# Layer 1's gate product as three 256-column matmuls summed in one PSUM region, and one more probability buffer in the attention of a two-layer block

## The chip, the cores and the metric

The kernel runs on one core of a Trainium2 chip. The metric is the device time of one execution in microseconds, and the time of a kernel is the median of several executions. The engines are named as the profile names them: PE (TensorE, matmul), PEld (the loads of PE's stationary operand, which overlap its matmuls), DVE (VectorE), ACT (ScalarE), POOL (GpSimd) and SP (SyncE, which here only issues DMAs). Each engine works through its own instructions in order.

## The reference, cut to what matters

A block of two layers works on 256 tokens and on 256 context tokens of width 2048. Layer 0 is a Fourier mixer, and layer 1 is attention with a window, a sink and a gate. What the change touches is in layer 1:

```
q, k, v, z = jnp.split(h @ w_in, [D_BRANCH, D_BRANCH + kvw, D_BRANCH + 2 * kvw], axis=-1)
...
p = jax.nn.softmax(jnp.concatenate([s, sk], axis=-1), axis=-1)[..., :-1]
o = jnp.einsum('bhgqk,bkhd->bqhgd', p, v)
y = o.reshape(b, n, D_BRANCH) * jax.nn.silu(z)
x = x + gate * (y @ w_out[i])
```

`h` has 256 rows of 2048 numbers. `z` has 4096 columns. There are 64 heads of 64 columns each, and each head has 512 keys (256 of the sequence and 256 of the context) for 256 queries.

## The kernel before, in words

All weights come as float32 and are used in two parts. A cast on ACT (`wh`) keeps the high bits, and a subtraction on DVE (`wl`) keeps the rest; both parts have the type float32r. `half_split` (line 69) does that for a tile of 128 x 1024. The activations are kept in two parts in the same way: in layer 1, `hx1[k]` is a tile of 128 x 512 with the high part of 256 tokens in columns 0 to 255 and the low part in columns 256 to 511, for 16 tiles `k` of the 2048 inputs. A product in full precision is then three matmuls, high by high, high by low and low by high, which the helper `mm3` (line 144) issues; the product of the low parts is left out.

Layer 1's attention is one long loop over 66 slots (line 1556). Its parts are:

- `stage_s(i)` (line 1476) for head `i`. Per block `tb` of 128 queries, PE makes the scores (lines 1489 and 1490), DVE adds the mask and takes the maximum (line 1491), and ACT takes the exponential into `p` (line 1494). DVE makes the reciprocal of the sum. ACT then writes the high half of the scaled probabilities into `f` in float16 (line 1506), DVE writes the low half (line 1507), and SP issues a transposing DMA from `f` to `ft` (line 1509). There are two `f` and one `ft` per head; `f` has 3 buffers and `ft` has 3.
- `stage_o(i - 2)` (line 1519) for the head two slots earlier. PE multiplies the values with `ft` (lines 1524 and 1525), ACT copies the upper 64 rows to a small tile `ot` (line 1530, a tile of its own with one buffer), and DVE adds them to the lower 64 rows (line 1531).
- two fillers per slot, which are units of other matmul work taken from one list (`units`, line 1379). A unit is an eighth of a group's query product (`q`, 64 units), half of a gate block (`z`, 64 units for 32 blocks), or a part of the last output product (`o`, 14 units). Each unit needs one `half_split`, which is asked for one unit ahead (`prep`, line 1402), and there are six buffers for `wh` and `wl`.

A gate block `z` is 128 of the 4096 gate columns for 256 tokens. It is built from 16 tiles `k`. For each tile the kernel before issues two matmuls, which share one PSUM tile of 512 columns: `wh` against the whole `hx1[k]` (line 1451, 512 columns), so that high by high lands in columns 0 to 255 and high by low in columns 256 to 511, and `wl` against the high half (line 1453, 256 columns), which adds to columns 0 to 255. Behind the last tile the two halves are added: ACT copies the right half to a tile `zs` (line 1457), DVE adds the left half (line 1458), ACT takes a tanh (line 1459), and DVE makes the SiLU's product `th` (line 1460). `emit_y` (line 1466) multiplies that with the head's output.

The order of the work on each engine is fixed when the program is built. A planner takes the instructions as the source writes them, runs them through a timing model with the buffers that the pools have, and writes one list per engine. Tiles of one tag share the buffers of that tag, and the instruction that first writes a new tile waits for those that last used the buffer. The pool `act` (line 40) has 33 buffers of 128 x 512 and one common tag `act`: among others the tiles of the rotary step on POOL (lines 1132 to 1138), the 16 tiles `y1` and scratch tiles are taken from it.

Loads of weights (`raw`, line 47, 1 MB each, three buffers) and the transposing DMAs are both issued by SP, in one order. POOL's own work in this stage is the rotary step for the queries, the low part of the keys (line 1346), and a share of the splits of `y` (line 1274).

Of the kernel before, what the change touches and what calls it, by code (L numbers as in the profile page):

```python
# [10 lines left out]
F32 = mybir.dt.float32  # L11
F32R = mybir.dt.float32r
F16 = mybir.dt.float16
AF = mybir.ActivationFunctionType
ALU = mybir.AluOpType
AX = mybir.AxisListType

P = 128
D = 2048
KT = D // P  # L20
DB = 4096
NB = DB // P
N = 256
# [9 lines left out]
def tile_dit(ctx: ExitStack, tc: tile.TileContext, a: dict, out: bass.AP):  # L33
    nc = tc.nc
    V, S, PE, GP = nc.vector, nc.scalar, nc.tensor, nc.gpsimd
# [19 lines left out]
    def act(dt=F32):  # L55
        return actp.tile([P, 512], dt, tag="act", name="act")
# [87 lines left out]
    def mm3(o, wh, wl, xh, xl, start, stop):  # L144
        PE.matmul(o, wh, xh, start=start, stop=False)  # L145
        PE.matmul(o, wh, xl, start=False, stop=False)  # L146
        return PE.matmul(o, wl, xh, start=False, stop=stop).ins  # L147
# [491 lines left out]
    for g in range(G):  # L639
        for j in {13: (8, 9), 14: (10, 11)}.get(g, (g - 5,) if 5 <= g < 13 else ()):  # L640
            t = up.tile([P, 1024], F32, name="pz", tag="pz", bufs=1)
# [217 lines left out]
    with tc.tile_pool(name="yp", reuse_waits="tile", bufs=32) as ypool:  # L859
# [39 lines left out]
        if True:  # L899
# [21 lines left out]
            for kg in range(4):  # L921
# [10 lines left out]
                for j in range(4):  # L932
                    k = kg * 4 + j
                    wh, wl = w[j // 2]
                    for b in range(4):
                        q = slice((j % 2) * 512 + b * P, (j % 2) * 512 + (b + 1) * P)
# [7 lines left out]
            for b in range(4, NB):  # L944
# [9 lines left out]
                o = psum()  # L954
                for k in range(KT):
# [13 lines left out]
                    wh, wl = w[k // 8]  # L969
                    q = slice((k % 8) * P, (k % 8 + 1) * P)  # L970
# [60 lines left out]
        for i in range(32):  # L1031
            sw, kg = i // 16, i % 16
            if kg == 0:
                o = [psum() for _ in range(8)]
# [9 lines left out]
            if kg == 14:  # L1044
                q = gt0[:, sw * 8 : sw * 8 + 8].rearrange("p k s -> p (k s)")
# [12 lines left out]
            if kg >= 12:  # L1058
                for k in range(sw * 8 + (kg - 12) * 2, sw * 8 + (kg - 12) * 2 + 2):
                    t = act()  # L1060
# [6 lines left out]
            for j, b in [(j, b) for b in range(8) for j in range(2)] if edge else [(j, b) for j in range(2) for b in range(8)]:  # L1067
                q = slice(b * P, (b + 1) * P)
# [35 lines left out]
    with tc.issue_after(st_end[0]):  # L1104
        o = psum()
# [34 lines left out]
    with tc.tile_pool(name="h1", reuse_waits="tile", bufs=16) as h1p:  # L1140
        hx1 = []
# [3 lines left out]
        with tc.tile_pool(name="kvp", reuse_waits="tile", bufs=2) as kvp:  # L1145
# [4 lines left out]
            for k in range(KT):  # L1150
                z2 = kvp.tile([P, 1024], F16, tag="hz", name="hz", bufs=16)
                t = kvp.tile([P, 512], F32, tag="ht", name="ht")
                for s in range(2):
                    q = slice(s * N, (s + 1) * N)
# [40 lines left out]
            o = [[psum() for _ in range(2)] for _ in range(4)]  # L1195
            for kg in range(8):
# [16 lines left out]
                for j in range(2):  # L1213
                    k = kg * 2 + j
                    wh, wl = w[j]
                    for tb in range(4):
                        c = tb // 2 * 512 + tb % 2 * P
                        for kv in range(2):
                            q = slice(kv * 512, (kv + 1) * 512)
                            mm3(o[tb][kv], hz[k][:, c : c + P], hz[k][:, N + c : N + c + P], wh[:, q], wl[:, q], k == 0, k == KT - 1)  # L1220
            kr = []
            for tb in range(4):
                t, ab = act(), act(F32R)
# [3 lines left out]
                t = act()  # L1227
# [20 lines left out]
            for tb in range(4):  # L1248
                t = vs[tb][0]
# [10 lines left out]
        with tc.tile_pool(name="at", reuse_waits="tile", bufs=2) as at:  # L1260
# [152 lines left out]
            def emit_unit():  # L1413
                if pos[0] >= len(ulist):
                    return
                u = ulist[pos[0]]
                if pos[0] not in ready:
                    ready[pos[0]] = prep(u)
                if pos[0] + 1 < len(ulist):
                    ready[pos[0] + 1] = prep(ulist[pos[0] + 1])  # L1420
                w = ready.pop(pos[0])
                pos[0] += 1
                kind, n, i, o = u
                if kind == "o":
                    if n == 0:
                        oA.extend([psum(), psum()])
                    for j in range(2):
                        o1_step(n * 2 + j, oA, *(t[:, j * 512 : (j + 1) * 512] for t in w))
                    return
                wh, wl = w  # L1430
                if kind == "q":
                    if i == 0:
                        o += [psum(), psum()]
                    if (n, i) == (0, 4):
                        with tc.issue_after(last_cast[0]):
                            prep_kk(0)
                    for j in range(2):
                        k = i * 2 + j
                        q = slice(j * 512, (j + 1) * 512)
                        for tb in range(2):  # L1440
                            mm3(o[tb], hx1[k][:, tb * P : (tb + 1) * P], hx1[k][:, N + tb * P : N + (tb + 1) * P], wh[:, q], wl[:, q], k == 0, k == KT - 1)
                    if i == 7:
                        finish_q(n, o)
                else:
                    if i == 0:
                        o.append(psum())
                    for k in range(i * 8, i * 8 + 8):
                        q = slice((k % 8) * P, (k % 8 + 1) * P)
                        for part in (0, 1) if k < KT - 1 else (1, 0):
                            if part == 0:  # L1450
                                PE.matmul(o[0], wh[:, q], hx1[k], start=k == 0, stop=k == KT - 1)  # L1451
                            else:
                                PE.matmul(o[0][:, 0:N], wl[:, q], hx1[k][:, 0:N], start=False, stop=False)  # L1453
                    if i == 1:
                        th = at.tile([P, N], F32, tag="th", name="th", bufs=3)
                        zs = at.tile([P, N], F32, tag="zs", name="zs", bufs=1)
                        S.copy(zs, o[0][:, N : 2 * N])
                        V.tensor_tensor(zs, o[0][:, 0:N], zs, op=ALU.add)
                        S.activation(th, zs, AF.Tanh, scale=0.5)
                        V.scalar_tensor_tensor(th, th, 1.0, zs, op0=ALU.add, op1=ALU.mult)  # L1460
                        szs[n] = th
                        emit_y(n)
# [13 lines left out]
            def stage_s(i):  # L1476
                hk, blk, hh = i // 8, i // 2, i % 2
                p2, pr = (blk % 4) // 2, blk % 2
                kkh, kkl = kk[hk]
                q2 = qq[hk, p2][hh]  # L1480
                pt = [at.tile([P, 512], F32, tag="p", name="p", bufs=3) for _ in range(2)]
                mx = at.tile([P, 2], F32, tag="mx", name="mx")
                sm = at.tile([P, 2], F32, tag="sm", name="sm")
                es = at.tile([P, 2], F32, tag="es", name="es")
                so = []
                for tb in range(2):
                    o = psum()
                    st = q2[:, (pr * 2 + tb) * P : (pr * 2 + tb + 1) * P]
                    PE.matmul(o, st, kkh, start=True, stop=False)  # L1489
                    PE.matmul(o, st, kkl, start=False, stop=True)  # L1490
                    V.tensor_tensor_reduce(o, o, mask[:, tb, :], -0.125, nsink[:, i : i + 1], ALU.add, ALU.min, mx[:, tb : tb + 1])  # L1491
                    so.append(o)
                for tb in range(2):
                    S.activation(pt[tb], so[tb], AF.Exp, bias=mx[:, tb : tb + 1], scale=-1.0, accum_out=sm[:, tb : tb + 1])  # L1494
                S.activation(es, mx, AF.Exp, bias=sink[:, i : i + 1])
                V.scalar_tensor_tensor(sm, sm, 1.0 / PS, es, op0=ALU.mult, op1=ALU.add)
                V.reciprocal(sm, sm)
                ft = at.tile([P, 8, 2, P], F16, tag="ft", name="ft", bufs=3)
                fs = []
                for tb in range(2):  # L1500
                    if i < 61:
                        f = at.tile([P, 1024], F16, tag="f", name="f", bufs=3)
                    else:
                        f = actp.tile([P, 1024], F16, tag="act", name="f")
                        fs.append(f)
                    fa = S.activation(f[:, 0:512], pt[tb], AF.Copy, scale=sm[:, tb : tb + 1]).ins  # L1506
                    f_last[:] = fa, V.scalar_tensor_tensor(f[:, 512:1024], pt[tb], sm[:, tb : tb + 1], f[:, 0:512], op0=ALU.mult, op1=ALU.subtract).ins  # L1507
                    if i < 61:
                        nc.sync.dma_start_transpose(ft[:, :, tb, :], f)
                return ft, fs  # L1510
# [8 lines left out]
            def stage_o(i, ft, fs):  # L1519
                hk, blk, hh = i // 8, i // 2, i % 2  # L1520
                oo = psum()
                for kb in range(4):
                    fh, fl = (ft[:, j, :, :].rearrange("p t q -> p (t q)") for j in (kb, 4 + kb))
                    PE.matmul(oo[:, 0:N], v01[kb][:, hk, :], fh, start=kb == 0, stop=False)  # L1524
                    PE.matmul(oo[:, 0:N], v01[kb][:, hk, :], fl, start=False, stop=kb == 3)  # L1525
                if hh == 0:
                    obs[blk, 0] = at.tile([P, N], F32, tag="ob", name="ob", bufs=4)
                ob = obs[blk, 0]
                t = at.tile([64, N], F32, tag="ot", name="ot", bufs=1)
                S.copy(t, oo[64:128, 0:N])  # L1530
                V.tensor_tensor(ob[hh * 64 : hh * 64 + 64, :], oo[0:64, 0:N], t, op=ALU.add)
                if hh == 1:
                    obs[blk, 1] = ob
                    emit_y(blk)
# [21 lines left out]
            for i in range(66):  # L1556
# [3 lines left out]
                if i == 61:  # L1560
                    t = actp.tile([P, 1024], F16, tag="act", name="ident16")
# [15 lines left out]
        with tc.tile_pool(name="fin", reuse_waits="tile", bufs=1) as fp:  # L1577
# [42 lines left out]
            for kg in range(16):  # L1620
# [10 lines left out]
                for j in range(2):  # L1631
                    k = kg * 2 + j
# [188 lines left out]
```

## Time and profile before

| what | us |
|---|---|
| median of 3 runs | 1764.61 (1764.34 to 1765.5) |
| the profiled execution, its own time | 1766.34 |
| its span from the first to the last instruction | 1764.5 |
| PE busy | 1728.8 (98%) |
| DVE busy | 1421.9 (81%) |
| ACT busy | 1148.4 (65%) |
| first and last matmul of the gate product (line 1451) | 1142.7 and 1567.0 |

A row of a group gives the line, the engine, the operation, the tiles (out <- in), the sizes and the number of instructions. Behind the bar it gives the busy time and the mean length of one in ns, and behind the second bar the time that the engine was idle just before such an instruction, with what ended the idle time. A row of the timeline gives the start, the length, the engine, the line and the operation. Matmuls are pipelined: the length of one reaches to the modelled end of its results, so the next one starts earlier than that, and the rate of PE is read from starts and not from lengths.

### The profile page before, as it was taken

How to read it: one execution, taken by the hardware profiler on the slowest of the kernel's cores; microseconds unless marked ns; L12 is line 12 of the kernel's file. 1: busy time of each engine (PE TensorE's matmuls, PEld its weight loads, DVE VectorE, ACT ScalarE, POOL GpSimd, SP SyncE). 2: the span in 40 equal slices, each digit the busy share in tenths (PEclk: the TensorE clock that was granted, in tenths of full speed). 3: DMA queues.
4: the chain of work that ended last, by engine and by line, in shares of the span. 5: the costliest groups of instructions: out<-in, count | busy, mean ns of one | idle time of the engine just before them, and what ended most of it. 6: DMA issues, size and time to landing. Idle time of an engine off the chain costs nothing.

```text
span 1764.5 us, 26891 instructions
## 1 busy us (share of the span) xinstructions
PE 1728.8 (98%) x9539; PEld 1149.6 (65%) x9539; DVE 1421.9 (81%) x2475; ACT 1148.4 (65%) x2197; POOL 361.3 (20%) x485
## 2 busy tenths in 40 slices
PE   6999999999999999999999999999999999999998
PEld 4679999644444444446444745788888878877464
DVE  5769888798676787777698686899899889998755
ACT  5545556476777755465235596688888788897643
POOL 0002111211222105212311111412303221251001
PEclk9999999999999999999999999999999999999999
DMA  9998999778998869977996594688997897888643
GB/s 394 417 342 254 275 273 257 295 282 303 340 314 299 312 227 378 372 254 258 394 341 229 181 362 155 191 198 198 222 212 200 204 212 207 210 192 283 225 172 120
DMA packets 232296, 465.66 MB, mean 264 GB/s; under 512 B 154497, under 2 KB 154897, under 8 KB 205281
## 3 DMA queue, kind: packets, MB, share of 16 engines
q1 hardware_dynamic: 180672, 331.41, 58.5%
q0 software_dynamic: 47344, 125.58, 22.2%
q10 hardware_dynamic: 4144, 6.95, 1.2%
q8 instruction: 75, 1.23, 0.3%
q14 instruction: 61, 0.49, 0.1%
HBM read 419.30 MB, written 12.59 MB: 245 GB/s over the span
## 4 chain that ended last, share of the span: by engine, by line
PE 80%; DVE 8%; DMA 7%; ACT 3%; issue 2%; POOL 0%; POOLq 0%; ACTq 0%; DVEq 0%; SPq 0%
PE ps L145 23%; PE ps L146 23%; PE ps L147 22%; PE ps L1451 3%; DMA ft<-f 3%; DMA raw<-in_awp 2%; PE ps L1453 2%; DVE wl L67 2%; DVE f L1507 1%; PE ps L286 1%; DVE ps L1491 1%; PE ps L1489 1%; PE ps L1490 1%; PE ps L1524 1%; PE ps L1525 1%
## 5 line engine op out<-in xcount | busy, mean ns | idle before, releaser
L67 DVE TENSOR_TENSOR wl<-raw,wh 128x1024 fp32r<-128x1024 f32 x152 | 203.1, 1337 | 38.4 <-ACT wh L66 27.2
L146 PE MATMUL ps<-act,wf 128*128 128x512 f16 x512 | 194.0, 379 | 0.0
L147 PE MATMUL ps<-act,wf 128*128 128x512 f16 x512 | 191.1, 379 | 0.0
L145 PE MATMUL ps<-act,wf 128*128 128x512 f16 x512 | 189.8, 379 | 0.6 <-ACT wf L137 0.3
L66 ACT CAST wh<-raw 128x1024 fp32r<-128x1024 f32 x152 | 158.2, 1042 | 48.0 <-PE ps L146 29.1
L1451 PE MATMUL ps<-h,wh 128*128 128x512 f32 x512 | 184.8, 397 | 0.0
L145 PE MATMUL ps<-y,wf 128*128 128x512 f16 x448 | 169.8, 379 | 0.8 <-ACT wf L137 0.8
L146 PE MATMUL ps<-y,wf 128*128 128x512 f16 x448 | 169.8, 379 | 0.0
L147 PEld LDWEIGHTS <-wf 128*128 128x128 f16 x960 | 93.9, 98 | 113.3
L145 PEld LDWEIGHTS <-wf 128*128 128x128 f16 x960 | 93.7, 98 | 113.2 <-ACT wf L137 4.2
L147 PE MATMUL ps<-y,wf 128*128 128x512 f16 x448 | 164.9, 379 | 0.0
L146 PEld LDWEIGHTS <-wf 128*128 128x128 f16 x960 | 93.9, 98 | 109.0
L137 ACT ACTIVATE wf<-raw,nrm 128x1024 f16<-128x1024 f32 x56 | 63.5, 1145 | 130.1 <-PE ps L147 78.6
L1453 PE MATMUL ps<-h,wl 128*128 128x256 f32 x512 | 138.7, 281 | 0.3 <-DVE wl L67 0.3
L138 DVE SCALAR_TENSOR_TENSOR wf<-raw,tn,wf 128x1024 f16<-128x1024 f32 x64 | 79.8, 1281 | 42.5 <-ACT wf L137 41.8
L1494 ACT ACTIVATE p<-ps,mx 128x512 f32<-128x512 f32 x128 | 88.1, 689 | 39.7 <-DVE mx L1491 36.6
L829 ACT ACTIVATE act<-act 128x512 f32<-128x512 f32 x178 | 109.4, 616 | 5.9 <-DMA act<-in_wo 4.5
L790 POOL DMA_DIRECT2D wa<-in_adw x64 | 34.2, 535 | 371.7 <-PE ps L147 144.9
L1507 DVE SCALAR_TENSOR_TENSOR f<-p,sm,f 128x512 f16<-128x512 f32 x128 | 103.5, 829 | 8.3 <-ACT f L1506 8.0
L1451 PEld LDWEIGHTS ps<-h,wh 128*128 128x128 f32 x512 | 96.2, 188 | 18.9
L1506 ACT ACTIVATE f<-p,sm 128x512 f16<-128x512 f32 x128 | 88.0, 717 | 31.1 <-DMA ft<-f 18.4
L146 PE MATMUL ps<-wl,h 128*128 128x512 f32 x256 | 101.8, 398 | 0.6 <-DVE wl L67 0.6
(430 smaller groups left out, 4863.6 us busy)
## 6 DMA issues: line engine op xcount, KB each, us to landing
raw<-in_wz SPq DMA_DIRECT2D x64, 1024.0 KB, 5.9
raw<-in_awp SPq DMA_DIRECT2D x32, 1024.0 KB, 12.7
zr<-in_adw SPq DMA_DIRECT2D x64, 512.0 KB, 7.0
wa<-in_adw POOLq DMA_DIRECT2D x64, 512.0 KB, 6.6
act<-in_wo POOLq DMA_DIRECT2D x128, 256.0 KB, 7.7
raw<-in_wo SPq DMA_DIRECT2D x32, 1024.0 KB, 8.2
raw<-in_wq SPq DMA_DIRECT2D x32, 1024.0 KB, 5.3
raw<-in_wu SPq DMA_DIRECT2D x32, 1016.0 KB, 6.7
```

What stands on the lines that cost most here:

```text
L66: last_cast[0] = S.copy(h, src).ins
L67: last_sub[0] = eng.tensor_tensor(l, src, h.bitcast(F32), op=ALU.subtract).ins
L138: last_sub[0] = V.scalar_tensor_tensor(w[:, 1], src, up, w[:, 0], op0=ALU.mult, op1=ALU.subtract).ins
L145: PE.matmul(o, wh, xh, start=start, stop=False)
L146: PE.matmul(o, wh, xl, start=False, stop=False)
L147: return PE.matmul(o, wl, xh, start=False, stop=stop).ins
L829: S.activation(t, t, AF.Square, accum_out=c)
L1451: PE.matmul(o[0], wh[:, q], hx1[k], start=k == 0, stop=k == KT - 1)
L1453: PE.matmul(o[0][:, 0:N], wl[:, q], hx1[k][:, 0:N], start=False, stop=False)
L1494: S.activation(pt[tb], so[tb], AF.Exp, bias=mx[:, tb : tb + 1], scale=-1.0, accum_out=sm[:, tb : tb + 1])
L1506: fa = S.activation(f[:, 0:512], pt[tb], AF.Copy, scale=sm[:, tb : tb + 1]).ins
L1507: f_last[:] = fa, V.scalar_tensor_tensor(f[:, 512:1024], pt[tb], sm[:, tb : tb + 1], f[:, 0:512], op0=ALU.mult, op1=ALU.subtract).ins
```

## The change

Three things change, and all lie in the attention loop of layer 1.

1. The gate product is made by `mm3` with 256 columns per matmul: `wh` by the high half, `wh` by the low half, and `wl` by the high half, all into columns 0 to 255 of the PSUM tile. The tile `zs`, the copy that filled it and the addition are gone. The tanh and the product behind it read the sum in PSUM.
2. `f`, the scaled probabilities of a head, has four buffers in place of three.
3. The tile `ot` with its own tag is gone. Its place is taken by a part of a tile of the common pool `act`.

The bytes per partition of the attention's pool stay the same: `zs` and `ot` gave back 1 KB each, and the fourth `f` takes 2 KB.

```diff
@@ -1446,16 +1446,10 @@
                     for k in range(i * 8, i * 8 + 8):
                         q = slice((k % 8) * P, (k % 8 + 1) * P)
-                        for part in (0, 1) if k < KT - 1 else (1, 0):
-                            if part == 0:
-                                PE.matmul(o[0], wh[:, q], hx1[k], start=k == 0, stop=k == KT - 1)
-                            else:
-                                PE.matmul(o[0][:, 0:N], wl[:, q], hx1[k][:, 0:N], start=False, stop=False)
+                        mm3(o[0][:, 0:N], wh[:, q], wl[:, q], hx1[k][:, 0:N], hx1[k][:, N : 2 * N], k == 0, k == KT - 1)
                     if i == 1:
                         th = at.tile([P, N], F32, tag="th", name="th", bufs=3)
-                        zs = at.tile([P, N], F32, tag="zs", name="zs", bufs=1)
-                        S.copy(zs, o[0][:, N : 2 * N])
-                        V.tensor_tensor(zs, o[0][:, 0:N], zs, op=ALU.add)
+                        zs = o[0][:, 0:N]
                         S.activation(th, zs, AF.Tanh, scale=0.5)
                         V.scalar_tensor_tensor(th, th, 1.0, zs, op0=ALU.add, op1=ALU.mult)
@@ -1499,7 +1493,7 @@
-                        f = at.tile([P, 1024], F16, tag="f", name="f", bufs=3)
+                        f = at.tile([P, 1024], F16, tag="f", name="f", bufs=4)
@@ -1526,7 +1520,7 @@
-                t = at.tile([64, N], F32, tag="ot", name="ot", bufs=1)
+                t = act()[0:64, 0:N]
                 S.copy(t, oo[64:128, 0:N])
                 V.tensor_tensor(ob[hh * 64 : hh * 64 + 64, :], oo[0:64, 0:N], t, op=ALU.add)
```

The helper that is now called, as it stands at line 144:

```
def mm3(o, wh, wl, xh, xl, start, stop):
    PE.matmul(o, wh, xh, start=start, stop=False)
    PE.matmul(o, wh, xl, start=False, stop=False)
    return PE.matmul(o, wl, xh, start=False, stop=stop).ins
```

## The prediction

> **What bounds the kernel now.** I read the page's busy times first, then the busy times by stretch, then PE's groups with their idle time, then the waits, and last PE's timeline.
>
> ```profile
> span 1764.5 us, 26891 instructions
> PE 1728.8 (98%) x9539; PEld 1149.6 (65%) x9539; DVE 1421.9 (81%) x2475; ACT 1148.4 (65%) x2197; POOL 361.3 (20%) x485
> ```
>
> PE is busy nearly all the time. The stage of the change runs from the first gate matmul to the end of the heads, 1142 to 1640 us. The next rows give the busy times of that stretch, and of two short ones: 283.19 to 286.07 is layer 0 where it issues `mm3` with 256 columns, and 1227.07 to 1229.51 is a gate unit.
>
> ```profile
> core 0: us, PE busy (x) PEld busy (x) DVE busy (x) ACT busy (x) POOL busy (x), PEclk, DMA share, GB/s
> 1142.00:1640.00 498.00, 492.81 (x2703) 402.94 (x2702) 458.63 (x839) 411.26 (x814) 124.56 (x100) 1.00 0.85 213
> ...
> 283.19:286.07 2.88, 2.88 (x26) 2.88 (x25) 2.80 (x4) 1.92 (x2) 0.00 (x0) 1.00 0.99 410
> 1227.07:1229.51 2.44, 2.44 (x16) 2.15 (x15) 2.33 (x6) 1.77 (x4) 0.00 (x0) 1.00 0.36 74
> ```
>
> In the stage PE is idle 498.00 - 492.81 = 5.2 us. DVE is idle 39 us (busy 92%) and ACT 87 us. So the stage goes at PE's pace, and DVE comes close behind it. The reader should see here how little there is to win: what PE does not wait for can't be given back. PE's groups in the same stretch say what the 5.2 us are:
>
> ```profile
> L1451 PE MATMUL ps<-h,wh 128*128 128x512 f32 x512 | 184.8, 397 | 0.0
> L1453 PE MATMUL ps<-h,wl 128*128 128x256 f32 x512 | 138.7, 281 | 0.3 <-DVE wl L67 0.3
> L146 PE MATMUL ps<-wl,h 128*128 128x512 f32 x192 | 76.3, 397 | 0.6 <-DVE wl L67 0.6
> ...
> L1524 PE MATMUL ps<-ft,v 128*128 128x256 f16 x252 | 59.0, 275 | 3.0 <-DMA ft<-f 2.1 <-DVE ft L1517 0.8
> ...
> L146 PE MATMUL ps<-wl,ys 128*128 128x512 f32 x64 | 25.6, 400 | 0.8 <-DVE wl L67 0.8
> ...
> L1370 PE MATMUL ps<-ident,act 128*128 128x128 f32 x56 | 8.6, 273 | 0.5 <-POOL act L1138 0.5
> ```
>
> So 2.1 us go to probabilities that were not transposed yet, 0.3 + 0.6 + 0.8 = 1.7 us to low weight parts from DVE, and 1.3 us to the rotary step on POOL and to the transposes by PE at the end. The waits of the same stretch give the counts:
>
> ```profile
> ACT f L1506 <- DMA ft<-f: 18.4, 23, 2.1
> ...
> ACT th L1459 <- DVE zs L1458: 3.2, 5, 1.0
> ...
> PE ps L1524 <- DMA ft<-f: 2.1, 4, 1.2
> ...
> PE ps L146 <- DVE wl L67: 1.4, 3, 0.8
> ...
> PE ps L1453 <- DVE wl L67: 0.3, 1, 0.3
> ```
>
> PE has 4 waits for `ft` and 3 + 1 for `wl`. The idle column counts only from the modelled end of the matmul before. In the timeline the largest wait reads:
>
> ```profile
> 1163.41 0.40 PE L1453 MATMUL ps<-h,wl 128*128 128x256 f32 x2
> 1163.65 0.40 PE L1451 MATMUL ps<-h,wh 128*128 128x512 f32 x1
> 1165.24 0.27 PE L1524 MATMUL ps<-ft,v 128*128 128x256 f16 x1 [1.20 <-DMA ft<-f]
> ```
>
> From start to start these are 1.59 us, of which a 512-column matmul takes 0.23 (next rows). 1.36 us are lost and 1.20 shown, so 0.16 us come on top of each wait: the 8 waits for `ft` and `wl` cost 3.8 + 8 x 0.16 = 5.1 us.
>
> **Part 1: the matmuls.** The first rows are the start of a gate unit and its eighth tile, seven tiles later; the two behind them are the starts of two triples in layer 0, eight triples apart.
>
> ```profile
> 1227.07 0.40 PE L1451 MATMUL ps<-h,wh 128*128 128x512 f32 x1
> 1227.30 0.28 PE L1453 MATMUL ps<-h,wl 128*128 128x256 f32 x1
> 1227.42 0.39 PE L1451 MATMUL ps<-h,wh 128*128 128x512 f32 x1
> ...
> 1229.51 0.39 PE L1451 MATMUL ps<-h,wh 128*128 128x512 f32 x1
> ```
>
> ```profile
> 283.19 0.28 PE L145 MATMUL ps<-act,wmh 128*127 128x256 f32 x1
> ...
> 286.07 0.28 PE L145 MATMUL ps<-act,wmh 128*127 128x256 f32 x1
> ```
>
> A tile takes (1229.51 - 1227.07) / 7 = 0.3486 us now: 0.23 for 512 columns and 0.1186 for 256. As a triple it streams the same 768 columns in three matmuls in place of two. Three times 0.1186 is 0.356; layer 0's triples take (286.07 - 283.19) / 8 = 0.360. Were only columns to count it would stay 0.3486. There are 32 blocks x 16 = 512 tiles, so the price lies at 0, +3.7 or +5.8 us. I take +4.7, between the last two: one is the 256-column matmul in its own place, the other the same three calls of the same helper, with 127 stationary columns and a DMA share of 0.99 around it. Nothing hides this cost, since PE is the bound.
>
> The Trainium skill ("TensorE: Matmul & The Clock Gate", section "Back-to-back issue gap") gives N / 2.4 + 2.5 ns for a matmul of N columns in the warm state. By it 512 more matmuls would cost 512 x 2.5 ns = 1.3 us, an estimate. The rows here disagree for float32: 256 columns take 118.6 ns and not 109, so the extra per matmul is larger and I keep 4.7.
>
> **Part 1, the sum behind it.** These rows are the gate's last steps and the head's:
>
> ```profile
> L1457 ACT COPY zs<-ps x32: 360/373/377, 1149.1 to 1573.3; 128x256 f32<-128x256 f32 x32
> L1458 DVE TENSOR_TENSOR zs<-ps,zs x32: 403/411/420, 1151.9 to 1575.5; 128x256 f32<-128x256 f32 x32
> ...
> L1460 DVE SCALAR_TENSOR_TENSOR th<-th,zs x32: 403/420/960, 1154.2 to 1588.2; 128x256 f32<-128x256 f32 x32
> ```
>
> ACT loses 32 x 0.373 = 11.9 us of work and DVE 32 x 0.411 = 13.2 us. Both had idle time, so none of it is a gain by itself; it is worth what PE's waits for DVE shrink. The tanh and the product now read PSUM. The same DVE operation elsewhere took 478 ns without and 476 ns with a PSUM operand, so I cost that at nothing:
>
> ```profile
> L1156 DVE SCALAR_TENSOR_TENSOR ht<-act,adab 128x256 f32<-128x256 f32 x30 | 12.6, 478 | 0.3 <-ACT act L1165 0.3
> ...
> L1156 DVE SCALAR_TENSOR_TENSOR ht<-act,adab,ps 128x256 f32<-128x256 f32 x2 | 0.9, 476 | 0.6 <-PE ps L1116 0.6
> ```
>
> The PSUM tile was let go after copy and addition, and now after tanh and product, which are as many steps on the same engines.
>
> **Part 2: the fourth `f`.** ACT waited 23 times, 18.4 us in all, 0.8 us on average, for a transposing DMA to give `f` back. Those waits go. ACT had 87 us to spare; what PE gets is an earlier start of the next transposes. That does not make a slow landing faster, and the largest wait of PE was one: SP spent 9.13 us on four transposes behind a weight load, and one landing takes up to 7.8 us.
>
> ```profile
> 1156.33 0.33 SPq L50 DMA_DIRECT2D raw<-in_wq  x1
> 1157.03 9.13 SPq L1509 DMA_TRANSPOSE ft<-f  x4
> ...
> DMA to landing us min/median/max: 3.0/5.1/7.8
> ```
>
> In SP's queue the weight loads stand behind the transposes. If `f` is ready earlier they go out earlier too, and no queue is passed. What is late next is the DMA itself, at a share of 0.85.
>
> Of the 5.1 us that parts 1 and 2 could give back I take a little under half, 2.3 us: the largest wait is a slow landing, and three of the four waits for `wl` lie at line 146, the products of queries and outputs, where no gate step is removed. The ends are 0 and 5.1.
>
> **Part 3: `ot` in the common pool.** Before, its buffer came from the addition of the head before; now it may be one that POOL has just used. I cost it at nothing: the addition frees it as soon as before, and the pool has 33 buffers. If it isn't free, ACT waits (second rival).
>
> **The sum.** +4.7 - 2.3 = +2.4 us. The profiled execution took 1766.34 us, its span and 1.8 us around it, so its like would take 1768.7. It stands 1.7 us above the median of the runs shown; against the median, 1764.61 + 2.4 = 1767.0 us. The work behind 1640 us has no gate matmul and moves as a whole. A measurement of this kernel can't tell less than about 0.2%, 3.5 us, from no change, so my forecast is no change, on the slow side.
>
> **The rivals.**
>
> *The load of the stationary operand decides.* In the layer 0 triples PEld is busy 2.88 of 2.88 us; in the gate unit 2.15 of 2.44. If the third load of every tile fills PEld, the triple takes 0.360 us, and PE's waits stay as they are: +5.8 us, no gain, 1770.4. Against it: PEld's overlapping loads count as busy without delaying PE. It is decided where a triple takes 0.358 us or more. The Trainium skill ("Trainium Kernel Development and Optimization", section "Performance Expectations") calls the busy share of weight loads, and not that of matmuls, the good measure of nearness to the limit; by that rule this rival is the outcome. In the stage PEld is busy 403 of 498 us before the third load comes.
>
> *`ot` waits for POOL, slower still.* The rotary step runs on tiles of the same pool:
>
> ```profile
> L1138 POOL TENSOR_TENSOR act<-act,rt 128x512 f32<-128x512 f32 x14 | 21.9, 1579 | 0.1
> ```
>
> If the copy to `ot` gets a buffer that POOL uses last, ACT stands still for up to 1.58 us, and behind it the casts of the weights and the next `f`. With 14 such instructions and half a microsecond of each reaching PE this is +7 on top of +2.4: 1774.0. It decides from about 0.1 us per slot. Against it: 33 buffers, and POOL is idle three quarters of the stage (124.56 of 498 busy).
>
> *The waits all go and only columns count.* 0 - 5.1 us: 1759.5. For it speaks that DVE has 13.2 us less to do and that `f` is never held; against it both rows of part 1.
>
> **How the numbers follow.** Forecast 0.54, loads 0.22, `ot` 0.14, all waits gone 0.08, and 0.02 for anything else slower. Faster by over 0.2% is the third rival, 0.08; slower the first two and the rest, 0.38; the same 0.54. The range leaves out the third rival and most of the second: 1762.5 to 1772.5. The forecast alone runs from 1763.2 (+3.7 and all 5.1 us given back) to 1768.1 (+5.8 and 2.3 given back).
>
> **What would show it.** The matmuls' step: starts of the first of each triple 0.356 to 0.360 us apart. The sum: DVE busy some 13 us less in the stage, ACT 12. The fourth `f`: no wait of line 1506's work for DMA. PE's idle time in the stage: 3 us. `ot`: no wait of its copy for POOL. The prediction is wrong if the planner's lists for ACT and DVE change so that `f` or `wl` come late in other places; then PE's waits for them grow beyond 5 us.

## The result, and the profile after

The changed kernel takes 1762.12 us (median of 15 runs, 1758.56 to 1764.42) against 1764.61 us for the kernel before, measured beside it. The ratio is 0.9983, with a 95% interval from 0.9976 to 0.9989. It is 0.17% faster: less than the 0.2% that the prediction set as its bound, but clear of zero, and below the range. Measured again, beside e9 and e11, it gave 1761.62 against 1764.62, ratio 0.9983 (0.9974 to 0.9991). The ratio on record is not the quotient of the two medians, and the two can differ a little (in e7 they are 0.9990 and 0.9978); a difference in us is one of medians.

The page after, in the lines that answer to those shown of before:

```profile
span 1761.0 us, 27814 instructions
PE 1728.4 (98%) x10051; PEld 1175.6 (67%) x10051; DVE 1404.9 (80%) x2443; ACT 1140.7 (65%) x2165; POOL 355.9 (20%) x485
```

PE has 512 matmuls more and is not busy for longer. DVE and ACT have 32 instructions fewer each. The busy times of the stage by stretch, with the same columns as before:

```profile
1142.00:1640.00 498.00, 495.95 (x3230) 430.10 (x3230) 445.87 (x809) 408.34 (x787) 122.95 (x103) 1.00 0.82 213
```

PE's idle time in it is 498.00 - 495.95 = 2.05 us, where it was 5.2. The groups of PE in the same stretch show what is left of it:

```profile
L145 PE MATMUL ps<-h,wh 128*128 128x256 f32 x512 | 145.9, 285 | 0.0
L146 PE MATMUL ps<-h,wh 128*128 128x256 f32 x512 | 143.0, 279 | 0.0
L147 PE MATMUL ps<-h,wl 128*128 128x256 f32 x512 | 142.9, 279 | 0.0
...
L146 PE MATMUL ps<-wl,h 128*128 128x512 f32 x192 | 75.8, 395 | 0.0
L1518 PE MATMUL ps<-ft,v 128*128 128x256 f16 x252 | 59.0, 275 | 2.1 <-DMA ft<-f 2.1
L146 PE MATMUL ps<-wl,ys 128*128 128x512 f32 x64 | 25.5, 398 | 0.0
...
L1370 PE MATMUL ps<-ident,act 128*128 128x128 f32 x56 | 8.4, 272 | 0.0
```

The reader should see zeros as the idle time of the other groups, where before there were 0.3, 0.6, 0.8 and 0.5. The waits for a low weight part from DVE are gone from these rows, and so is the one for POOL. What stays is the wait for `ft`. Nearly all of it is one wait at the end of the stage; a second one, as large, lies ahead of 1142 us and was there before (the first head's transposes). In PE's timeline they are:

```profile
1139.38 0.27 PE L1518 MATMUL ps<-ft,v 128*128 128x256 f16 x1 [2.03 <-DMA ft<-f]
```

```profile
1593.78 0.28 PE L1518 MATMUL ps<-ft,v 128*128 128x256 f16 x1 [1.78 <-DMA ft<-f]
```

A triple of the gate product, at its place (PE's timeline, four triples from the first to the last row):

```profile
1207.43 0.28 PE L145 MATMUL ps<-h,wh 128*128 128x256 f32 x1
1207.55 0.28 PE L146 MATMUL ps<-h,wh 128*128 128x256 f32 x1
1207.66 0.28 PE L147 MATMUL ps<-h,wl 128*128 128x256 f32 x1
1207.78 0.28 PE L145 MATMUL ps<-h,wh 128*128 128x256 f32 x1
...
1208.83 0.28 PE L145 MATMUL ps<-h,wh 128*128 128x256 f32 x1
```

That is (1208.83 - 1207.43) / 4 = 0.350 us per tile, against 0.3486 for the pair in the unit that the prediction shows.

The steps behind the gate, by their tile:

```profile
L1453 ACT ACTIVATE th<-ps x32: 377/384/386, 1149.4 to 1578.4; 128x256 f32<-128x256 f32 x32
L1454 DVE SCALAR_TENSOR_TENSOR th<-th,ps x32: 400/413/419, 1153.6 to 1582.6; 128x256 f32<-128x256 f32 x32
```

Where the time of the profiled executions went can be read from three marks: the first score matmul, the last start of the value product's first matmul (line 1524 before, 1518 after), which belongs to the last head, and the end of the span. Before they lie at 1128.7, 1622.7 and 1764.5 us, after at 1127.2, 1619.1 and 1761.0. The stage between the first two took 494.0 and takes 491.9. The part ahead of it is the same work in both kernels and differs by 1.5 us between single executions, which is no effect of the change; the part behind it takes 141.8 and 141.9. So of the 3.5 us between these two executions 2.1 belong to the stage.

One difference between the two executions is neither work nor a wait. Behind the wait for the first head's `ft`, PE ran at half its rate for a while in the execution after, and did not in the one before. The rows are neighbouring value products of that head, after and then before, and the stretch of the execution after by its busy times (the granted clock is the third number from the right):

```profile
1139.83 0.42 PE L1519 MATMUL ps<-ft,v 128*128 128x256 f16 x1
1140.05 0.42 PE L1518 MATMUL ps<-ft,v 128*128 128x256 f16 x1
```

```profile
1141.19 0.27 PE L1525 MATMUL ps<-ft,v 128*128 128x256 f16 x1
1141.30 0.27 PE L1524 MATMUL ps<-ft,v 128*128 128x256 f16 x1
```

```profile
1139.60:1142.90 3.30, 3.30 (x14) 2.59 (x12) 2.46 (x6) 1.73 (x5) 0.64 (x1) 0.50 0.98 338
```

The products start 0.22 us apart in the one and 0.11 in the other, at a granted clock of 0.50 and of 1.00, and the matmuls of this stretch take about 1.6 us more than at their usual spacing. Both profiled executions of the changed kernel have such a stretch there, as have those of e2, e3, e5 and e7 to e11; those of before, e1 and e4 do not. The wait ahead of it is 1.97 to 2.05 us in all of them, so its length doesn't tell them apart, and what does is not shown. With the same clock in both, the stage would be some 3.7 us shorter and not 2.1, an estimate from these two executions.

### The profile page after: what moved, and what is told of

Its sections match the earlier page's. It is cut to its first block, busy times and chain, and to the rows that moved or that the text cites. A ratio compares the mean times of both kernels' runs of the same rounds, so it can differ in the third digit from the quotient of the medians.

```text
span 1761.0 us, 27814 instructions
## 1 busy us (share of the span) xinstructions
PE 1728.4 (98%) x10051; PEld 1175.6 (67%) x10051; DVE 1404.9 (80%) x2443; ACT 1140.7 (65%) x2165; POOL 355.9 (20%) x485
## 4 chain that ended last, share of the span: by engine, by line
PE 75%; DVE 3%; ACT 1%; DMA 1%; issue 1%; POOLq 0%; ACTq 0%; POOL 0%; DVEq 0%
PE ps L145 23%; PE ps L146 23%; PE ps L147 22%; PE ps L1483 2%; PE ps L1484 2%; PE ps L1518 2%; PE ps L1519 1%; DMA ft<-f 1%; ACT wf L137 0%; ACT act L877 0%; DVE wl L67 0%; DVE wf L138 0%; DVE act L984 0%; DVE act L878 0%; PE ps L1370 0%
## 5 line engine op out<-in xcount | busy, mean ns | idle before, releaser
L145 PE MATMUL ps<-h,wh 128*128 128x256 f32 x512 | 145.9, 285 | 0.0
L146 PE MATMUL ps<-h,wh 128*128 128x256 f32 x512 | 143.0, 279 | 0.0
L147 PE MATMUL ps<-h,wl 128*128 128x256 f32 x512 | 142.9, 279 | 0.0
L1485 DVE CUSTOM_DVE_ANT_0 ps<-ps,mask,nsink 128x512 f32<-128x512 f32 x128 | 94.7, 753 | 11.2 <-PE ps L1484 10.7
## 6 DMA issues: line engine op xcount, KB each, us to landing
raw<-in_awp SPq DMA_DIRECT2D x32, 1024.0 KB, 12.7
```

## The experiments

The theory formed from the two profiles (called A in the expectations): the third matmul costs next to nothing, and the gain is PE's waits for DVE's results, which go because the sum behind the gate is gone. Its rivals were that the fourth buffer of `f` gives the gain (B), and that any edit gives the engines new lists, and the time moves by some microseconds by chance (C). All ratios are against the kernel before on the same chip.

| run | part | median us | ratio to before (95%) |
|---|---|---|---|
| e1 | three matmuls, sum kept | 1766.59 | 1.0008 (0.9999 to 1.0016) |
| e2 | matmuls as before, no sum | 1760.53 | 0.9970 (0.9960 to 0.9980) |
| e3 | part 1 alone | 1761.53 | 0.9980 (0.9971 to 0.9989) |
| e7 | all but the fourth `f` | 1761.26 | 0.9990 (0.9980 to 1.0000) |
| e4 | fourth `f`, `ot` and `zs` in the pool | 1775.77 | 1.0071 (1.0056 to 1.0085) |
| e5 | `ot` in the pool alone | 1769.72 | 1.0025 (1.0016 to 1.0034) |
| e8 | part 1 with a copy on ACT | 1760.97 | 0.9979 (0.9970 to 0.9988) |
| e10 | part 1 with a copy on DVE | 1767.28 | 1.0013 (1.0004 to 1.0021) |
| e9 | the change, fillers first in two slots | 1761.43 | 0.9981 (0.9972 to 0.9990) |
| e11 | part 1, fillers first in two slots | 1761.28 | 0.9976 (0.9966 to 0.9986) |

The median of before was 1765.11 us beside e1, e2, e3 and e7, 1764.88 beside e4, e5, e8 and e10, and 1764.62 beside e9, e11 and the repeated change.

### e1: the three matmuls, with the sum kept

```diff
-                        for part in (0, 1) if k < KT - 1 else (1, 0):
...
+                        PE.matmul(o[0][:, 0:N], wh[:, q], hx1[k][:, 0:N], start=k == 0, stop=False)
+                        PE.matmul(o[0][:, N : 2 * N], wh[:, q], hx1[k][:, N : 2 * N], start=False, stop=False)
+                        PE.matmul(o[0][:, 0:N], wl[:, q], hx1[k][:, 0:N], start=False, stop=k == KT - 1)
```

> The gate product alone goes to three 256-column matmuls; high by low still lands in the right half of the PSUM tile, and the copy and the addition stay, as do three buffers of f and the tile ot. Theory A (the third matmul costs little: a triple of the changed kernel starts every 0.350 us against 0.348 for a pair): +1 us, so within 0.1% of the kernel before, with PE waiting for wl and ft as before (some 5 us idle in the stage). The prediction's step (0.356 to 0.360 us per tile): +4 to +6 us, 0.2 to 0.3% slower. Theory C (any new order of the lists moves the time by some us by chance): up to 3 us either way, with PE's idle time in the stage changed.

It is 0.08% slower (1766.59 against 1765.11), at the edge of what the interval can tell from nothing. The stage took 493.7 us against 494.0 of before, both without the stretch at half clock. The price of the matmuls, with whatever the new lists add or give back, is about 1.5 us, and 4 to 6 us lies outside the interval (its upper bound of 1.0016 is 2.8 us).

### e2: the matmuls as before, without the sum

```diff
-                        zs = at.tile([P, N], F32, tag="zs", name="zs", bufs=1)
-                        S.copy(zs, o[0][:, N : 2 * N])
-                        V.tensor_tensor(zs, o[0][:, 0:N], zs, op=ALU.add)
+                        zs = o[0][:, 0:N]
```

> The matmuls stay as before (512 and 256 columns); the copy and the addition behind them are gone and the tanh reads the left half of the PSUM tile, so the high by low part of the gate product is left out of the result. Three buffers of f, and the tile ot. Theory A (the gain is PE's waits, which shrink because DVE and ACT have 13 and 12 us less to do): 2.5 to 4 us faster than before, PE's idle time in the stage down from 5 to 2 or 3 us. Theory B (the fourth f gives the gain): no change within 1 us, the waits of ACT for the DMA stay at some 18 us and PE's waits for ft too. The prediction: 1 to 2 us faster.

It is 0.30% faster by the ratio and 4.6 us by the medians, a little more than theory A asked for. ACT's waits for the DMA grew. PE's waits for `wl` went, and so did the one for the copy of the last heads' `ft` on DVE (0.8 us before, line 1517). The waits of its stage:

```profile
ACT f L1504 <- DMA ft<-f: 25.9, 24, 3.3
...
PE ps L1522 <- DMA ft<-f: 1.9, 4, 0.9
```

So ACT may wait 25.9 us for a buffer of `f` in the fastest kernel of this study. The removed sum alone is worth more than the whole change, by the medians. Since it leaves a part of the product out, it is no candidate for a faster kernel.

### e3: part 1 alone

```diff
...
+                        mm3(o[0][:, 0:N], wh[:, q], wl[:, q], hx1[k][:, 0:N], hx1[k][:, N : 2 * N], k == 0, k == KT - 1)
...
-                        zs = at.tile([P, N], F32, tag="zs", name="zs", bufs=1)
-                        S.copy(zs, o[0][:, N : 2 * N])
-                        V.tensor_tensor(zs, o[0][:, 0:N], zs, op=ALU.add)
+                        zs = o[0][:, 0:N]
```

> Part 1 of the change alone: three 256-column matmuls without the sum behind them; f keeps three buffers and ot its own tile. Theory A: 1.5 to 3 us faster than before, near the whole change. Theory B (the fourth f gives the gain): 0 to +1 us, and PE waits for ft as before. The prediction: +3 us.

0.20% faster, 3.6 us: at least the whole change. It is near what e1 and e2 give together (+1.5 and -4.6 us are -3.1). e1 and e3 make the same number of matmuls of the same size (in e1 the second of each three lands in the other half of the PSUM tile) and differ in the sum, and they lie 5.1 us apart on the same chip. Their lists on PE hardly differ: the value products of 57 of the 64 heads stand at the same place in both, and the others within 6 matmuls of it. The busy times of its stage and the waits for `ft`:

```profile
1142.00:1640.00 498.00, 497.35 (x3234) 431.08 (x3233) 443.88 (x812) 408.60 (x786) 117.70 (x100) 1.00 0.82 214
```

```profile
ACT f L1500 <- DMA ft<-f: 6.5, 11, 1.7
...
PE ps L1518 <- DMA ft<-f: 0.4, 1, 0.4
```

PE is idle for 0.65 us. ACT's waits for the DMA went from 18.4 to 6.5 us with three buffers of `f` still. They don't follow the sum alone, though: e2 has no sum either, and there they grew to 25.9 us.

### e7: the change without the fourth buffer

```diff
-                        f = at.tile([P, 1024], F16, tag="f", name="f", bufs=4)
+                        f = at.tile([P, 1024], F16, tag="f", name="f", bufs=3)
```

> The whole change but for the fourth f, which goes back to three buffers; ot lies in the common pool. Theory A: as part 1 alone, 1.5 to 3 us faster than before; if ot in the common pool costs nothing, the same as that run within 0.5 us. Theory B: 0 to +1 us. If the copy to ot waited for POOL it would show as a wait of line 1524's copy and as a slower run than part 1 alone.

The lists of all five engines are the same, line by line and operation by operation, as those of the changed kernel. So this pair differs in the waits alone, which makes it the cleanest test of part 2. The median is 1761.26 us and the ratio 0.9990 (0.9980 to 1.0000), against 0.9983 for the change; the intervals overlap. The runs lie in two groups, six at 1760.2 to 1761.3 us and five at 1763.4 to 1769.4, and the profiled one (1765.01) is of the second. ACT waits 7.0 us for the DMA where the change has none:

```profile
ACT f L1500 <- DMA ft<-f: 7.0, 8, 2.0
...
PE ps L1518 <- DMA ft<-f: 3.3, 1, 3.3
```

The one wait of PE is that at the end of the stage. It was 1.8 us in the first and 2.8 us in the second profiled execution of the changed kernel, so 3.3 us here may be the same thing. In this execution a second stretch at half clock follows it. A gain of the fourth buffer can't be told from nothing, and by the intervals it is no more than some 0.2%.

### e4: the fourth buffer without part 1

```diff
-                        zs = at.tile([P, N], F32, tag="zs", name="zs", bufs=1)
+                        zs = act()[:, 0:N]
...
-                        f = at.tile([P, 1024], F16, tag="f", name="f", bufs=3)
+                        f = at.tile([P, 1024], F16, tag="f", name="f", bufs=4)
...
-                t = at.tile([64, N], F32, tag="ot", name="ot", bufs=1)
+                t = act()[0:64, 0:N]
```

> Parts 2 and 3 without part 1: f has four buffers, the gate product and its sum are as before, and to make room ot and zs both lie in tiles of the common pool. Theory A (all of the gain is the sum's): no change within 1.5 us; ACT's waits for the DMA go from 18 us to none, and PE's waits for wl stay at 1.5 to 2 us. Theory B (the fourth f gives the gain): 2 to 3 us faster. Theory C (chance of the new lists): up to 3 us either way.

It is 0.71% slower by the ratio and 10.9 us by the medians, which none of the theories expected. ACT has no wait for the DMA left, as expected, and yet PE waits far more, in the same stretch:

```profile
PE ps L1524 <- DMA ft<-f: 9.0, 11, 1.9
PE ps L1524 <- DVE ft L1517: 4.9, 1, 4.9
```

So the fourth buffer showed no gain without part 1. The loss can't be put down to the buffer, since two tiles moved as well and the lists are new, and for the same reason this run alone would not rule theory B out. e3 does: the gain is whole with three buffers.

### e5: `ot` in the common pool alone

```diff
-                t = at.tile([64, N], F32, tag="ot", name="ot", bufs=1)
+                t = act()[0:64, 0:N]
```

> Part 3 alone: ot lies in the common pool, nothing else is changed. Theory A: no change within 1 us, and no wait of the copy to ot for POOL; as an edit that removes no work it also shows how far new lists alone move the time. The prediction's second rival: slower by up to 7 us, with waits of that copy for POOL.

0.25% slower by the ratio, 4.8 us by the medians. No wait of the copy for POOL shows in its trace. What changed are the lists: by line and operation, 379 of DVE's 2475 instructions and 330 of ACT's 2197 stand at another place than before, and on PE the value products of some heads stand up to 16 matmuls earlier or 27 later. PE's waits for `ft` grew, in the same stretch:

```profile
PE ps L1524 <- DMA ft<-f: 5.3, 6, 2.2
...
PE ps L146 <- DVE wl L67: 1.3, 2, 0.9
```

The longest of these waits, 2.17 us at 1600.84 us, is followed by a second stretch at half clock, which takes about 1.5 us more. So theory C has its share: an edit that removes no work moved this kernel by 0.25%, and its trace shows nothing else than the lists for it. With part 1 the same edit moves little (e3 without it 0.9980, e7 with it 0.9990).

### e8 and e10: a copy put back on ACT, or on DVE

```diff
                         zs = at.tile([P, N], F32, tag="zs", name="zs", bufs=1)
+                        S.copy(zs, o[0][:, 0:N])
```

```diff
                         zs = at.tile([P, N], F32, tag="zs", name="zs", bufs=1)
+                        V.tensor_scalar(zs, o[0][:, 0:N], 1.0, None, op0=ALU.mult)
```

Both start from e3 and let tanh and product read `zs` again.

> Part 1 alone with ACT's share of the sum put back: the triple writes the full sum in PSUM, ACT copies it to zs (0.37 us, 32 times), and tanh and product read zs; DVE makes no addition. If DVE's 13 us are what counts: still 3 to 4 us faster than the kernel before, as part 1 alone. If ACT's 12 us count as much: half of that gain, 1.5 to 2 us.

> Part 1 alone with DVE's share of the sum put back: DVE copies the full sum from PSUM to zs (about 0.41 us, 32 times), and tanh and product read zs; ACT makes no copy. If DVE's 13 us are what counts: the gain of part 1 is gone, 0 to +1.5 us against the kernel before, and PE waits for wl some 1.5 us again. If ACT's 12 us count as much: 1.5 to 2 us faster than before.

With ACT's copy the gain stays whole: 0.9979. With DVE's copy it is gone: 1.0013, 2.4 us slower than before. The two kernels do the same matmuls and the same number of instructions and differ in the engine of one copy, and they lie 6.3 us apart. Their lists differ too, but little on PE: the value products of 49 of the 64 heads stand at the same place in both, and all but one of the others within 5 matmuls of it. In the stage of the first, and then of the second (busy times by stretch):

```profile
1142.00:1640.00 498.00, 496.29 (x3231) 430.46 (x3230) 449.15 (x811) 416.60 (x815) 119.56 (x100) 1.00 0.84 213
```

```profile
1142.00:1640.00 498.00, 491.57 (x3201) 426.93 (x3200) 448.26 (x836) 401.06 (x776) 127.10 (x99) 1.00 0.83 210
```

PE is idle 1.7 us in the one and 6.4 us in the other, at nearly equal busy times of DVE in this window. The copies are 32 x 0.414 = 13.2 us of DVE's work in e10, but the window is fixed, and the stage ends 6.3 us later there; in e8 some of the products behind the tanh also took longer (19.4 us for the 32, against 15.6). What PE waits for in the second is the old list, `ft` and `wl`:

```profile
PE ps L1519 <- DMA ft<-f: 4.0, 5, 1.8
...
PE ps L146 <- DVE wl L67: 1.9, 3, 0.8
```

By this pair it is DVE's work that counted, and ACT's did not. The table says the same: every kernel without a step of DVE between the gate's matmuls and the tanh has a ratio of 0.9970 to 0.9990, and every changed one with such a step has 1.0008 to 1.0071.

### e9 and e11: both fillers ahead of the two waits that are left

```diff
                 filler()
+                if i in (2, 62):
+                    filler()
                 if i >= 2:
                     stage_o(i - 2, *pts.pop(i - 2))
-                filler()
+                if i not in (2, 62):
+                    filler()
```

> The changed kernel, with both fillers ahead of the head's output product in slots 2 and 62 alone, where PE still waits 2.0 and 1.8 us for ft. If the time in this stage is PE's work and PE's waits and nothing else: 2 to 4 us faster than the changed kernel, 4.5 to 7 us faster than the kernel before. If the two waits only move to the next head: as the changed kernel. The new lists may cost some us either way.

> Part 1 of the change alone (f keeps three buffers, ot its own tile), with both fillers ahead of the head's output product in slots 2 and 62. PE waits there 2.0 and 0.4 us: 1.5 to 2.5 us faster than part 1 alone, 5 to 6 us faster than the kernel before. If the waits only move: as part 1 alone, 3 to 3.6 us faster than before.

> The changed kernel itself, on the same chip as the two others. By its first runs: 2 to 4 us faster than the kernel before, and PE's waits for ft in the stage only at its start and its end.

e9 took 1761.43 us and the changed kernel beside it 1761.62: no gain. e11 took 1761.28 us, 0.24% below before by the ratio, and has the lowest ratio of the kernels that compute the whole result. But it cannot be told from part 1 alone (0.9980) or from the change (0.9983). The wait at the end of the stage is gone in e11, where part 1 alone had 0.4 us of it, and in e9 0.98 us of it are left, at 1594.85 us. The one at the start of the stage stays in both: PE's first product with `ft` comes at the same time, 1139.29 us in e9, with 1.98 us idle ahead of it. The edit in the source did not move it in PE's list. In e9 a new wait of 0.70 us came up at 1164.81.

## Why the prediction was wrong

The prediction said no change, on the slow side (+2.4 us), and the range began at 1762.5. The kernel got faster by 2.5 us. Each of the two large terms of the sum was off, in the same direction, and a third was not priced at all.

**The price of the matmuls (+4.7 us) was too high.** The step named three values, 0, +3.7 and +5.8, and took the middle of the upper two. The unit shown after has 0.350 us per triple, which is 512 x 0.0014 = +0.7 us against the pair of the unit before. Over all tiles that follow one another in a unit (some 450 in each trace) the median is 350 ns for the triple and 347 for the pair, which is 512 x 0.003 = +1.5 us. e1 measured +1.5 us for the kernel too (between 0 and 2.8 us by its interval). Layer 0's 0.360 was not the rate of these matmuls; why its triples are slower was not tried. The other value came from 0.3486 - 0.23, where the 0.23 carries two digits: an error of 0.002 there is threefold in the triple, and 3 us in the sum. The triples of the trace after give 0.117 per matmul and not 0.1186. The estimate from the Trainium skill ("TensorE: Matmul & The Clock Gate", section "Back-to-back issue gap"), 1.3 us, came closer than the sum, and the trace agrees with it in size.

**The waits given back (-2.3 of at most 5.1 us) were too few.** The 5.1 us were the bound from above, and the runs came close to all of it. e2, which removes the sum and nothing else, gained 4.6 us. PE's idle time in the stage fell from 5.2 to 2.05 us in the change and to 0.65 us in e3. The reason given for taking less than half was that the waits for `wl` lie at units where no gate step is removed, and that one landing was slow. The first is true and does not matter: DVE works in order, so a gate step taken out makes everything behind it earlier, in the next unit too. The statement "both had idle time, so none of it is a gain by itself" read DVE by its mean, 92% busy. e8 and e10 show what it hid: 13 us of DVE's work spread over the stage were worth 6.3 us of the kernel's time, and 12 us of ACT's work nothing that can be told. With the measured sizes the sum is +1.5 - 4.6 = -3.1 us, near the -2.5 and -3.0 us that the changed kernel gave.

One way in which that reaches PE can be worked out from the trace, for the 61 heads whose transposes go by DMA. I took the start of the first score matmul, the end of DVE's second write to `f`, the later landing of the two transposes, and the start of the first product with `ft`, and averaged over the heads:

| kernel | scores to `f` written, us | transpose issued to landed, us | landed to used, us | heads used less than 0.2 us after landing |
|---|---|---|---|---|
| before | 12.7 | 4.8 | 1.4 | 7 |
| the change | 10.0 | 4.7 | 3.8 | 3 |
| e1 (three matmuls, sum kept) | 12.3 | 4.7 | 2.0 | 7 |
| e2 (no sum) | 12.2 | 4.7 | 1.9 | 6 |
| e3 (part 1) | 10.7 | 4.6 | 3.5 | 4 |
| e8 (copy on ACT) | 10.4 | 4.7 | 3.6 | 3 |
| e10 (copy on DVE) | 12.7 | 4.7 | 1.7 | 11 |
| e5 (`ot` alone) | 14.0 | 4.5 | 1.3 | 13 |
| e4 (fourth `f`) | 14.9 | 4.7 | 1.0 | 17 |

The DMA takes about the same time in all of them. What differs is how long a head's chain takes through DVE and ACT, and in most rows a longer chain goes with more heads that come just in time or late. e2 does not fit: it is the fastest kernel, and its chain is nearly as long as that of before and as that of e1, 6 us above it. What went in e2 are PE's waits for `wl` (1.7 us before) and for the copy of `ft` on DVE (0.8 us). So the head's chain is one way from DVE's work to PE's waits and these are another, and how much each carries is not shown.

The largest wait of the prediction, at 1165 us, was read as a slow landing, and it was one: the fourth head's second transpose landed 6.8 us after its issue. In the changed kernel the same transpose took 3.1 us, and PE did not wait for it. The next head's took 7.5 us there, and of that 0.28 us were left as a wait (PE's timeline after):

```profile
1169.21 0.27 PE L1518 MATMUL ps<-ft,v 128*128 128x256 f16 x1 [0.28 <-DMA ft<-f]
```

**The fourth `f`.** Costed with part 1 as a share of the 2.3 us. It did what it says, ACT's waits for the DMA went from 18.4 us to none, and by e7 that was worth nothing that can be told. ACT's waits were on an engine with 87 us to spare, as the prediction noted, and in e3 most of them went without it.

**`ot` in the common pool, costed at nothing.** The rival's mechanism, a wait for POOL, did not show in any run. But by itself the edit cost 4.8 us (e5), by its trace through the lists. The prediction named this possibility as what would make it wrong and gave it no price; with 4.8 us for an edit without work it deserved more than the 0.02 for anything else, in both directions. In the changed kernel this price did not appear.

**The rivals.** That the loads of the stationary operand decide (0.22) is ruled out: the loads go on at 0.350 us per triple, though the rule of the Trainium skill on the busy share of loads ("Trainium Kernel Development and Optimization", section "Performance Expectations") pointed there; PEld is now busy 430.10 of 498 us without holding PE up. The third rival, that the waits go and only columns count, had 0.08 and was nearest in both its terms, with +1.5 for 0 and a gain of 3 to 5 us for 5.1; the time lies between its 1759.5 and the forecast.

**What held.** PE bounds the stage, and its time is PE's work and PE's waits, with one thing that the prediction did not have: the stretches at half clock, 1.5 to 1.6 us each in the profiled executions that have them. DVE lost 32 additions of 0.411 us; its busy time in the stretch fell from 458.63 to 445.87 us, the 13 us that were named. ACT's fell by 3 us and not by 12 in that stretch, and by 7.7 us over the whole program (1148.4 to 1140.7 us); what makes up the rest is not shown. Reading PSUM cost DVE nothing (0.413 us against 0.420).

What stays open: how the planner comes to put a product with `ft` earlier or later when only a tile's pool changes, and so how much of the change's own 2.5 us is the luck of its lists. That e1, e2, e3, e8 and e10 agree with one sum (+1 to +2 us for the matmuls, -4.6 to -6.3 for a step of DVE, nothing for ACT's copy) speaks for the mechanism and against luck, within about 2 us. Open too is what decides whether PE's clock is halved behind a wait of 2 us.

## What to carry to other kernels

Where the engine that feeds the bound one is nearly full (92% here) and works in order, a step taken out of its queue can be worth nearly all of the bound engine's waits, wherever these lie, and the same step on an engine with more room nothing (83% here). Test it by putting the step back on one engine and then on the other. A buffer that removed waits on an engine with room gave no gain that could be told here. In a kernel with planned lists an edit that takes away no work can move the time by more than the change under study, so each part needs a run of its own. And before two profiled executions are compared stage by stage, the granted clock of each stage is to be read: one stretch at half clock cost about 1.6 us where the change gained 2.5.

## What the runs showed of the hardware

A 256-column float32r matmul in a row of its like starts every 0.117 us, and a triple takes 0.350 us, the 768 columns' time of a 512 and a 256 (0.347 us) within 1%, though each of the three has a load of 128 columns of its own. The same calls in layer 0 took 0.360 us. ACT's tanh took 0.384 us with its input in PSUM and 0.417 us with it in SBUF (medians of 32 each), so dropping the tile `zs` also made the step behind it shorter. Behind a wait of 2.03 us PE's granted clock was 0.50 from 1139.6 to 1142.9 us in the changed kernel, and float16 products of 256 columns started 0.22 us apart in place of 0.11; behind a wait of 2.01 us in the kernel before it stayed at 1.00.
